# Thirty-two experts of a two-block model: one fixed stream on three engines, bias over 128 partitions, slot tables by fours

## The chip, the cores and the metric

The kernel runs on one core of one Trainium2 chip. The metric is the device time of one execution in microseconds (us); it is taken as the median of several runs. One further execution is recorded by the hardware profiler, and every row below comes from it.

## The reference, cut to what matters

The model has two blocks on 512 tokens of width 1024, in float32. The first mixes with sparse attention and a gated MLP and has a SwiGLU network; the second mixes with differential attention and a pooling mixer, then has a mixture of 32 experts, of which each token takes 4, and ends with a gated per-layer embedding. The change touches the expert stage alone:

```
logits = xt @ w_router + b_router
top_vals, top_idx = lax.top_k(logits, 4);  gates = softmax(top_vals)
# each expert e, on the rows xb of the tokens that chose it:
gt  = minimum(xb @ w_gate[e] + b_gate[e], 7.0)
up  = clip(xb @ w_up[e] + b_up[e], -7.0, 7.0)
hdn = (up + 1.0) * (gt * sigmoid(1.702 * gt))
y   = hdn @ w_down[e] + b_down[e]
# each token: sum of its four experts' rows y, weighted by gates
```

All three weights of an expert are 1024 x 1024, so the stage reads 32 x 3 x 4 MB.

## The kernel before

**Weights.** A weight of an expert comes in eight parts of 128 x 1024 (512 KB), each by one DMA on SP's queue. Products need float32 accuracy on a TensorE mode that takes a rounded operand, so every part is split (`split`, called by `load_part`; L282): ScalarE writes the rounded high half `whi` (a cast), VectorE the low half `wlo` (raw minus high). The rows `xe` (tokens) and `he` (hidden rows) are split in the same way after their transposes. `mm3` (L311 to L313) makes a product of three matmuls: high weight with high rows, low weight with high rows, high weight with low rows. A part of 1024 columns takes two halves of 512, so six matmuls.

**Buffers.** A planner (`W["plan"]`) hands out slots in rotation. At the experts there are 29 slots for raw parts and eight for halves, so the halves of a part lie in the slots of the part four before it: ScalarE's cast for part i + 4 waits until TensorE has finished the product of part i.

**An expert.** At most 112 rows (`CAP`). `prepare_slots` makes a one-hot table (`oh`, VectorE), multiplies it with the token table on TensorE and takes from the result (`sl`) the gate of each slot, and the row to gather (`gi`). `gather` fetches the rows into `xg` by an indirect DMA on POOL, `flipped` transposes and splits them. `add_bias` opens each PSUM bank with a matmul of one column of `pick`, repeated 112 times, against the bias, over 64 partitions: high and low half of the bias, 32 experts each. Gate and up parts alternate by pairs. Then the limit of the gate is taken by VectorE from PSUM in two halves (L1546, `gm`), ScalarE applies the gate function to `gm` (L1547), VectorE limits up in two halves (L1548, `uc`), and forms (up + 1) x gate (L1549). The down product of an expert is made after the gate and up products of the next; its result is scaled by ScalarE (`yt`, L1519) and added to the output rows by an indirect DMA.

**What sets the order.** Each engine works through its queue in order. The program order in the source is not that order: the Tile scheduler places each instruction by a priority and by its own estimates, so that parts of one expert mix with limits and transposes of another. Only a few places are fixed by hand with `hold`, a dependency without a semaphore.

Of the kernel before, what the change touches and what calls it, by code (L numbers as in the profile page):

```python
# [26 lines left out]
NEG = -1.0e30  # L27
NE = 32
CAP = 112
LAMBDA_INIT = 0.8 - 0.6 * math.exp(-0.3 * 0)  # L30
TWO_PI = (6.28125, 0.0019350051879882812, 3.019915981956752e-07)

# [192 lines left out]
def build(tc, I, out, dbg=None, stop=None):  # L225
# [3 lines left out]
    with es:  # L229
# [74 lines left out]
        def load_part(src, after=()):  # L304
            return start_part(src)(after)
# [1140 lines left out]
        turn = {"n": -1}  # L1446

        def part(src):
            n = turn["n"] = turn["n"] + 1
            return load_part(src, held if n <= 3 else ())  # L1450


        def expert_piece(src):
            return Piece([part(src[k * P:(k + 1) * P]) for k in range(2)])

        def expert_rows(ps, w, a, kp):
            for kk in range(2):
                k = 2 * kp + kk
                for c in range(2):
                    mm3(ps[c], (a[0][:, k], a[1][:, k]), w[kk * D + c * 512:kk * D + (c + 1) * 512], False, k == 7)  # L1460
# [9 lines left out]

        def slot_rows(pl, sl, n, bufs, m=P, norm=False):

            sg = pl.tile([P, n], F32, name="slot_gate", bufs=bufs)[:m]
            nc.vector.tensor_tensor(out=sg, in0=sl[:, :, 0], in1=sl[:, :, 1], op=ALU.add)
            rr = None
            if norm:
                rr = pl.tile([P, n], F32, name="slot_norm", bufs=1)[:m]
                nc.vector.tensor_tensor(out=rr, in0=sl[:, :, 3], in1=sl[:, :, 4], op=ALU.add)
            em = pl.tile([P, n], F32, name="empty", bufs=bufs)[:m]
            nc.vector.tensor_scalar(out=em, in0=sl[:, :, 2], scalar1=0.0, scalar2=10000.0, op0=ALU.is_equal, op1=ALU.mult)  # L1480
            gi = pl.tile([P, n], I32, name="gi", bufs=bufs)[:m]
# [3 lines left out]
        def prepare_slots(e0, n):  # L1485
            pt = ps_tr()
            for j in range(n):
                oh = one_hot(e0 + j) if e0 + j else oh0[0]
                for tt in range(NT):
                    W["pick"] = nc.tensor.matmul(pt[:CAP, 6 * j:6 * j + 6], oh[:, tt], info[:, tt, e0 + j], start=tt == 0, stop=tt == NT - 1)  # L1490
            sl = early.tile([P, n, 6], F32, name="sl", bufs=2)[:CAP]
            nc.vector.tensor_copy(sl.rearrange("p j c -> p (j c)"), pt[:CAP, :6 * n])
            *cols, last = slot_rows(early, sl, n, 6, CAP, e0 == 0)
# [4 lines left out]
        def flipped(a, name):  # L1498
# [13 lines left out]
        def down(e, he):  # L1512
            pd = [t[:CAP] for t in ps_mm()]
            add_bias(pd, e, 2)
            for kp in range(4):
                expert_rows(pd, expert_piece(I["we_down"][e, kp * 256:kp * 256 + 256]), he, kp)
            yt = row_tile("yt")[:CAP]
            last = W["mm"]
            halves(lambda cs, p: nc.scalar.activation(yt[:, cs], p, AF.Copy, scale=slots[e][0]), pd)  # L1519
            add_rows(yt, slots[e][1])  # L1520
            return last

        first = prepare_slots(0, 1)
        held = (W["gate"], first)
        normalize_first()
        prepare_slots(1, 1)

        ahead = [expert_piece(I["we_" + n][0, kp * 256:kp * 256 + 256]) for kp, n in ((0, "gate"), (0, "up"))]

        keep_warm(10, bias[:, 0, 0:P], bias[:, 0, 0:512], W["pick"])  # L1530
        xe = flipped(xg[:CAP], "xe")
        he = None
        for e in range(NE):
            if e + 1 < NE:
                gather(e + 1)
            pg, pu = [[t[:CAP] for t in ps_mm()] for _ in range(2)]
            add_bias(pg, e, 0)
            add_bias(pu, e, 1)
            for kp in range(4):
                rows = slice(kp * 256, kp * 256 + 256)  # L1540
                expert_rows(pg, ahead.pop(0) if ahead else expert_piece(I["we_gate"][e, rows]), xe, kp)
                expert_rows(pu, ahead.pop(0) if ahead else expert_piece(I["we_up"][e, rows]), xe, kp)
                if kp == 0 and e + 2 < NE:
                    prepare_slots(e + 2, 1)
            gm, uc = row_tile("gm")[:CAP], row_tile("uc")[:CAP]
            halves(lambda cs, p: nc.vector.tensor_scalar(out=gm[:, cs], in0=p, scalar1=7.0, scalar2=None, op0=ALU.min), pg)  # L1546
            nc.scalar.activation(gm, gm, AF.Gelu_apprx_sigmoid)  # L1547
            halves(lambda cs, p: nc.vector.tensor_scalar(out=uc[:, cs], in0=p, scalar1=7.0, scalar2=-7.0, op0=ALU.min, op1=ALU.max), pu)  # L1548
            nc.vector.scalar_tensor_tensor(out=uc, in0=uc, scalar=1.0, in1=gm, op0=ALU.add, op1=ALU.mult)  # L1549
            if e + 1 < NE:  # L1550
                xe = flipped(xg[:CAP], "xe")
            if he is not None:
                down(e - 1, he)
            he = flipped(uc, "he")
        last = down(NE - 1, he)
# [28 lines left out]
        def overflow_rows(op, e, r):  # L1584
# [26 lines left out]
                return t  # L1611

            def product(a, n):
                ps = [ps_b(), ps_b()]
# [35 lines left out]
        with pool("fin", 2, side="right") as wp:  # L1650
# [7 lines left out]
            for tt in range(NT):  # L1658
# [7 lines left out]
                ps = ps_mm()  # L1666
# [34 lines left out]
```

## Time and profile before

| | |
|---|---|
| median of 3 runs | 2238.23 us (2235.29 to 2238.75) |
| the profiled execution | 2236.76 us, span of its instructions 2235.0 us |
| TensorE matmul (PE) | 2156.0 us busy, 96% of the span |
| VectorE (DVE) | 1699.7 us, 76% |
| ScalarE (ACT) | 1372.4 us, 61% |
| GpSimd (POOL) | 199.2 us, 9% |
| granted TensorE clock, mean | 0.989 |

PE, DVE, ACT and POOL are the four computing engines; PEld is TensorE's weight load, which runs beside the matmuls; SP issues DMAs. A share of the span mixes stages: the first 920 us are the first block, the attention of the second block and the router; the experts take the time from about 920 to 2161 us; the gated embedding follows. So the table says which engine is busiest, not what a change in the expert stage is worth. The rows further down are taken from the expert stage alone. In a timeline row, the first number is the start in us from the beginning of the span, the second the duration (of a group: from the first start to the last end), and the square bracket tells how long the engine had been idle and what released it.

### The profile page before, as it was taken

The numbers are of one execution on the slowest core, as the hardware profiler recorded it, in microseconds if no ns is written. First come the engines' busy times: TensorE is split into PE (matmuls) and PEld (weight loads), VectorE is DVE, ScalarE is ACT, GpSimd is POOL, SyncE is SP. The second block draws the span as 40 slices with busy tenths as digits, with TensorE's granted clock in tenths as the row PEclk, the third lists the DMA queues.
The fourth block names the chain that finished last, engine by engine and source line by source line (L and its number), as shares of the span: only waits on it lengthen the run. The fifth ranks groups of instructions, "written<-read, shape, count | busy, mean of one in ns | idle before, by whom it ended". The sixth has DMA issues, their size and how long they took to land. (4 is left out here: it accounts for less than half of the span.)

```text
span 2235.0 us, 30297 instructions
## 1 busy us (share of the span) xinstructions
PE 2156.0 (96%) x10458; PEld 1658.2 (74%) x10459; DVE 1699.7 (76%) x2475; ACT 1372.4 (61%) x1873; POOL 199.2 (9%) x323
## 2 busy tenths in 40 slices
PE   9999999999999888899999999999999999999998
PEld 7777788888878777677777777777666676676667
DVE  6688772323677666799999999998888888888872
ACT  4666652222554553477777777777676676776762
POOL 0000110000003422100000000000000000000000
PEclk9999999999999999899999999999999999999999
DMA  5411744334663136799999999999999898898841
GB/s 208 152 29 37 256 151 142 94 96 159 196 204 111 29 104 220 276 348 345 359 341 362 336 361 343 356 323 348 322 330 344 300 343 323 326 345 299 309 134 67
DMA packets 159980, 543.77 MB, mean 243 GB/s; under 512 B 23107, under 2 KB 26179, under 8 KB 159820
## 3 DMA queue, kind: packets, MB, share of 16 engines
q1 hardware_dynamic: 138816, 500.63, 62.0%
q0 software_dynamic: 8192, 16.80, 3.2%
q10 hardware_dynamic: 12812, 24.35, 3.2%
q8 instruction: 84, 1.38, 0.3%
q14 instruction: 76, 0.62, 0.1%
HBM read 525.93 MB, written 28.33 MB: 248 GB/s over the span
## 5 line engine op out<-in xcount | busy, mean ns | idle before, releaser
L282 DVE TENSOR_TENSOR wlo<-wraw,whi 128x1024 fp32r<-128x1024 f32 x923 | 1096.7, 1221 | 226.7 <-ACT whi L282 209.8
L282 ACT CAST whi<-wraw 128x1024 fp32r<-128x1024 f32 x923 | 954.3, 1054 | 369.7 <-PE pa L313 122.5
L312 PE MATMUL pa<-wlo,he 128*112 128x512 f32 x504 | 202.3, 401 | 18.0 <-DVE wlo L282 18.0
L312 PE MATMUL pb<-wlo,xe 128*112 128x512 f32 x512 | 208.2, 407 | 0.0
L313 PE MATMUL pb<-whi,xe 128*112 128x512 f32 x512 | 201.3, 394 | 0.0
L313 PE MATMUL pa<-whi,he 128*112 128x512 f32 x504 | 198.0, 393 | 0.0
L311 PE MATMUL pa<-whi,he 128*112 128x512 f32 x504 | 188.5, 395 | 1.2 <-ACT he L282 1.2
L311 PE MATMUL pb<-whi,xe 128*112 128x512 f32 x512 | 185.9, 394 | 0.0
L312 PEld LDWEIGHTS pa<-wlo,he 128*112 128x112 f32 x504 | 87.9, 174 | 55.4 <-DVE wlo L282 27.0
L312 PEld LDWEIGHTS pb<-wlo,xe 128*112 128x112 f32 x512 | 89.3, 174 | 32.6 <-issue 7.9
L311 PEld LDWEIGHTS pa<-whi,he 128*112 128x112 f32 x504 | 87.7, 174 | 34.4 <-ACT whi L282 5.0
L311 PEld LDWEIGHTS pb<-whi,xe 128*112 128x112 f32 x512 | 89.4, 175 | 29.5 <-ACT xe L282 0.3
L313 PEld LDWEIGHTS pb<-whi,xe 128*112 128x112 f32 x512 | 89.4, 175 | 24.6 <-DVE xe L282 0.2
L311 PE MATMUL pa<-whi,xe 128*112 128x512 f32 x264 | 107.5, 407 | 0.0
L313 PEld LDWEIGHTS pa<-whi,he 128*112 128x112 f32 x504 | 87.9, 174 | 25.5
L312 PE MATMUL pa<-wlo,xe 128*112 128x512 f32 x264 | 106.4, 403 | 0.0
L313 PE MATMUL pa<-whi,xe 128*112 128x512 f32 x264 | 103.8, 394 | 0.0
L1509 POOL DMA_INDIRECT base<-yt,gi x32 | 47.7, 1489 | 567.7 <-DVE wlo L282 461.9
L313 PE MATMUL po<-whi,xe 128*112 128x512 f32 x248 | 97.7, 394 | 0.0
L312 PE MATMUL po<-wlo,xe 128*112 128x512 f32 x248 | 97.6, 394 | 0.0
L311 PE MATMUL po<-whi,xe 128*112 128x512 f32 x248 | 97.4, 393 | 0.0
L1418 POOL DMA_INDIRECT xg<-normed,gi x31 | 33.5, 1081 | 600.0 <-PE tr L345 570.2
(579 smaller groups left out, 4402.3 us busy)
## 6 DMA issues: line engine op xcount, KB each, us to landing
wraw<-in_we_gate_dram SPq DMA_DIRECT2D x256, 512.0 KB
wraw<-in_we_up_dram SPq DMA_DIRECT2D x256, 512.0 KB
wraw<-in_we_down_dram SPq DMA_DIRECT2D x256, 512.0 KB
wraw<-in_w_gu_dram SPq DMA_DIRECT2D x44, 512.0 KB
wraw<-in_w_down_dram SPq DMA_DIRECT2D x44, 512.0 KB
wraw<-in_w_out_dram SPq DMA_DIRECT2D x24, 512.0 KB
wraw<-in_w_v_dram SPq DMA_DIRECT2D x10, 512.0 KB
wraw<-in_w_uv_dram SPq DMA_DIRECT2D x8, 512.0 KB
```

The source lines that it names most:

```text
L282: return nc.scalar.copy(hi, src), nc.vector.tensor_tensor(out=lo, in0=src, in1=hi.bitcast(F32), op=ALU.subtract)
L311: nc.tensor.matmul(o, a[0], b[0], start=start, stop=False)
L312: nc.tensor.matmul(o, a[0], b[1], start=False, stop=False)
L313: W["mm"] = nc.tensor.matmul(o, a[1], b[0], start=False, stop=stop)
L1418: nc.gpsimd.indirect_dma_start(out=xg[:CAP], out_offset=None, in_=normed if e else base, in_offset=bass.IndirectOffsetOnAxis(ap=slots[e][1 ...
L1509: nc.gpsimd.indirect_dma_start(out=base, out_offset=bass.IndirectOffsetOnAxis(ap=ap, axis=0), in_=y_, in_offset=None, bounds_check=S - 1, ...
```

## The change

Nine things change, all in the expert stage:

1. The products are written as one sequence of parts: for each expert eight gate parts, eight up parts, then the eight down parts of the expert before. Parts are fetched so that three stand ahead of the one in use.
2. After the expert loop, every instruction of TensorE, VectorE and ScalarE of this stretch gets a dependency on the one before it on its engine (`behind`), so that the order in the source is the order in the queue.
3. `add_bias` takes all 128 partitions: `pick` has a second plane, with zeros in the partitions that belong to another bias, written by two memsets on POOL.
4. ScalarE applies the gate function directly to PSUM; the limit of the gate is put on the result, as a minimum with the function's value at 7 (`GELU_MAX`), inside the gated product.
5. The +1 of up is in its bias; its limits are then 8 and -6, taken in one instruction of 1024 columns.
6. PSUM for the experts is one pool of three tiles of 1024 columns.
7. The output rows `yt` are scaled in one instruction.
8. The slot tables of four experts are made together, with their one-hots spread over one expert's products.
9. Limits, splits of `xe` and `he` and output rows stand at fixed products q of an expert (q counts from 0 to 23).

```diff
+GELU_MAX = 7.0 / (1.0 + math.exp(-1.702 * 7.0))
...
-        pick = early.tile([P, NE], F32R, name="pick")
+        pick = early.tile([P, 2, NE], F32R, name="pick")
...
+        nc.gpsimd.memset(pick.bitcast(F32), 0.0)
+        nc.gpsimd.memset(bias[64:P, 1].bitcast(F32), 0.0)
         for q in range(4):
-            nc.vector.tensor_copy(pick[q * NE:(q + 1) * NE], ident[0:NE, 0:NE])
+            nc.vector.tensor_copy(pick[q * NE:(q + 1) * NE, q // 2], ident[0:NE, 0:NE])
...
-            nc.scalar.copy(bias[b:b + NE, h], braw)
-            nc.vector.tensor_tensor(out=bias[b + NE:b + 2 * NE, h], in0=braw, in1=bias[b:b + NE, h].bitcast(F32), op=ALU.subtract)
+            one = 1.0 if j == 1 else 0.0
+            nc.scalar.activation(bias[b:b + NE, h], braw, AF.Copy, bias=one)
+            nc.vector.scalar_tensor_tensor(out=bias[b + NE:b + 2 * NE, h], in0=braw, scalar=one, in1=bias[b:b + NE, h].bitcast(F32), op0=ALU.add, op1=ALU.subtract)
...
+        W["ps"].release()
+        W["ps"] = alloc("ps2", 1, space=PSUM)
+
+        def ps_wide():
+            return W["ps"].tile([P, D], F32, tag="w", name="pw", bufs=3)
+
+        def ps_pair():
+            t = ps_wide()
+            return [t[:, 0:512], t[:, 512:D]]
 
         def add_bias(ps, e, j):
             for c in range(2):
-                b = slice((j * 64) % P, (j * 64) % P + 64)
-                nc.tensor.matmul(ps[c], pick[b, e:e + 1].to_broadcast([64, CAP]), bias[b, j // 2, c * 512:(c + 1) * 512], start=True, stop=False)
+                nc.tensor.matmul(ps[:CAP, c * 512:(c + 1) * 512], pick[:, j % 2, e:e + 1].to_broadcast([P, CAP]), bias[:, j // 2, c * 512:(c + 1) * 512], start=True, stop=False)
 
...
+        def turned(a):
+            pts = []
+            for half in range(2):
+                pt = ps_tr()
+                for j in range(4):
+                    c = half * 4 + j
+                    nc.tensor.transpose(pt[:, j * CAP:(j + 1) * CAP], a[:, c * P:(c + 1) * P], ident[:CAP, :CAP])
+                pts.append(pt[:, :4 * CAP].rearrange("p (j t) -> p j t", j=4))
+            return pts
+        def halves_of(pts, name):
             t = [ep.tile([P, 8, CAP], F32R, name=f"{name}{q}") for q in range(2)]
-            transposed(a, t, slice(0, CAP), CAP)
+            for half, pt in enumerate(pts):
+                split(pt, *[q[:, 4 * half:4 * half + 4] for q in t])
             return t
...
+        seq = []
+        for e in range(NE):
+            seq += [("gate", e, k) for k in range(8)] + [("up", e, k) for k in range(8)]
+            seq += [("down", e - 1, k) for k in range(8)] if e else []
+        seq += [("down", NE - 1, k) for k in range(8)]
+        parts = []
+
+        def fetch(upto):
+            while len(parts) < min(upto, len(seq)):
+                n, e, k = seq[len(parts)]
+                parts.append(load_part(I["we_" + n][e, k * P:(k + 1) * P], held if len(parts) <= 3 else ()))
+
+        fetch(4)
...
+        def limited_gate():
+            hidden["g"] = row_tile("gm")[:CAP]
+            nc.scalar.activation(hidden["g"], hidden["pg"][:CAP], AF.Gelu_apprx_sigmoid)
+        def limited_up():
+            hidden["u"] = row_tile("uc")[:CAP]
+            nc.vector.tensor_scalar(out=hidden["u"], in0=hidden["pu"][:CAP], scalar1=8.0, scalar2=-6.0, op0=ALU.min, op1=ALU.max)
+        def gated_rows():
+            u = hidden["u"]
+            nc.vector.scalar_tensor_tensor(out=u, in0=hidden["g"], scalar=GELU_MAX, in1=u, op0=ALU.min, op1=ALU.mult)
+        def put_rows(e, ps):
+            yt = row_tile("yt")[:CAP]
+            nc.scalar.activation(yt, ps[:CAP], AF.Copy, scale=slots[e][0])
+            add_rows(yt, slots[e][1])
         for e in range(NE):
             if e + 1 < NE:
                 gather(e + 1)
+            batch = list(range(e + 2, min(e + 2 + NB, NE))) if e % NB == 0 else []
+            ohs, pts, pslot = {}, None, None
+            for q in range(24 if e else 16):
+                fetch(at["i"] + 4)
+                if q == 0:
+                    hidden["pg"] = ps_wide()
+                    add_bias(hidden["pg"], e, 0)
+                if q == 1 and e:
+                    operand["h"] = halves_of(turned_h, "he")
+                if q == 2 and pd is not None:
+                    put_rows(e - 2, pd)
+                    pd = None
+                if q in (0, 2, 6, 8) and len(ohs) < len(batch):
+                    ohs[len(ohs)] = one_hot(batch[len(ohs)])
+                if q in (4, 6, 10, 12):
+                    j = (4, 6, 10, 12).index(q)
+                    if j < len(batch):
+                        if j == 0:
+                            pslot = ps_tr()
+                        slot_products(pslot, j, ohs[j], batch[j])
+                if q == 13 and batch:
+                    slot_columns(pslot, batch[0], len(batch))
+                if q == 8:
+                    hidden["pu"] = ps_wide()
+                    add_bias(hidden["pu"], e, 1)
+                if q == 10:
+                    limited_gate()
+                if q == 16:
+                    pd = ps_wide()
+                    add_bias(pd, e - 1, 2)
+                if q == 17 and e + 1 < NE:
+                    operand["x"] = halves_of(pts, "xe")
+                if q == 18:
+                    limited_up()
+                if q == 19:
+                    gated_rows()
+                if q < 16:
+                    product(hidden["pg" if q < 8 else "pu"], operand["x"])
+                else:
+                    product(pd, operand["h"])
+                if q == 15 and e + 1 < NE:
+                    pts = turned(xg[:CAP])
+            if e == 0:
+                operand["x"] = halves_of(pts, "xe")
+                limited_up()
+                gated_rows()
+            turned_h = turned(hidden["u"])
...
+        behind = {}
+        for ins in list(traced[mark:]):
+            if ins.engine in ORDERED:
+                if ins.engine in behind:
+                    tc.add_manual_dep(ins, behind[ins.engine], mybir.DependencyInfo(mybir.DependencyClass.NoSync, mybir.DependencyReason.DATA), reason="order")
+                behind[ins.engine] = ins.name
...
```

On VectorE, in the middle of the expert stage, this is what stood in its queue from one expert's slot tables to the next `he` (`gm`, `uc`: gate and up rows; `wlo`: low halves of weight parts):

```order
L282 TENSOR_TENSOR wlo<-wraw,whi 128x1024 x8
L1546 TENSOR_SCALAR gm<-pa 112x512
L282 TENSOR_TENSOR wlo<-wraw,whi 128x1024
L1546 TENSOR_SCALAR gm<-po 112x512
L1548 TENSOR_SCALAR uc<-pb 112x512 x2
L282 TENSOR_TENSOR wlo<-wraw,whi 128x1024
L1549 SCALAR_TENSOR_TENSOR uc<-uc,gm 112x1024
L282 TENSOR_TENSOR xe_15734<-tr,xe_15733 128x448 x2
L282 TENSOR_TENSOR wlo<-wraw,whi 128x1024 x10
L282 TENSOR_TENSOR he_15856<-tr,he_15855 128x448 x2
```

and this stands there now (`pw` is a PSUM tile of 1024 columns):

```order
L285 TENSOR_TENSOR wlo<-wraw,whi 128x1024 x16
L285 TENSOR_TENSOR xe_15879<-tr,xe_15878 128x448 x2
L285 TENSOR_TENSOR wlo<-wraw,whi 128x1024
L1575 TENSOR_SCALAR uc<-pw 112x1024
L285 TENSOR_TENSOR wlo<-wraw,whi 128x1024
L1579 SCALAR_TENSOR_TENSOR uc<-gm,uc 112x1024
L285 TENSOR_TENSOR wlo<-wraw,whi 128x1024 x5
L1419 TENSOR_TENSOR oh<-iota,slot_of 128x448
L285 TENSOR_TENSOR wlo<-wraw,whi 128x1024
L285 TENSOR_TENSOR he_16002<-tr,he_16001 128x448 x2
```

The two gate limits are gone; the up limit and the gated product stand behind the split of `xe`, with one low half between each.

On TensorE, at the passage from one expert's up products to the down products of the expert before, these rows stood before (`tr`: transposes, `pa`, `pb`, `po`: PSUM banks of 512 columns):

```order
L311 MATMUL pb<-whi,xe_14641 112x512 x2
L1465 MATMUL pa<-bias,pick 112x512
L312 MATMUL pb<-wlo,xe_14641 112x512
L313 MATMUL pb<-whi,xe_14642 112x512
L312 MATMUL pb<-wlo,xe_14641 112x512
L313 MATMUL pb<-whi,xe_14642 112x512
L311 MATMUL pa<-whi,he_14763 112x512 x2
L1465 MATMUL po<-bias,pick 112x512
L1465 MATMUL pb<-bias,pick 112x512 x2
L312 MATMUL pa<-wlo,he_14763 112x512
```

and now:

```order
L315 MATMUL pw<-wlo,xe_15878 112x512
L316 MATMUL pw<-whi,xe_15879 112x512
L1511 MATMUL tr<-ident,xg 128x112 x8
L1467 MATMUL pw<-bias,pick 112x512 x2
L314 MATMUL pw<-whi,he_16001 112x512
L315 MATMUL pw<-wlo,he_16001 112x512
L316 MATMUL pw<-whi,he_16002 112x512
L314 MATMUL pw<-whi,he_16001 112x512
```

The biases no longer stand between a product's own matmuls; both of a tile follow the transposes or the product before.

## Rows read from the trace of the kernel before

**Rows 1.** Busy time by stretch; columns: window, length, busy us and counts of engines.

```profile
core 0: us, PE busy (x) PEld busy (x) DVE busy (x) ACT busy (x) POOL busy (x), PEclk, DMA share, GB/s
1100.00:1200.00 100.00, 100.00 (x455) 74.14 (x454) 93.81 (x104) 76.49 (x83) 5.97 (x5) 1.00 0.97 359
...
1700.00:1800.00 100.00, 97.00 (x431) 69.59 (x429) 88.19 (x99) 71.97 (x80) 6.45 (x5) 1.00 0.90 325
```

**Rows 2.** ScalarE's timeline: the gate function of three experts.

```profile
1193.82 1.06 ACT L1547 ACTIVATE gm<-gm 112x1024 f32<-112x1024 f32 x1
...
1456.12 1.05 ACT L1547 ACTIVATE gm<-gm 112x1024 f32<-112x1024 f32 x1
...
2133.70 1.06 ACT L1547 ACTIVATE gm<-gm 112x1024 f32<-112x1024 f32 x1 [4.96 <-DVE gm L1546]
```

**Rows 3.** Waits, 1500 to 2100: engine, line, releaser; total us, times, longest.

```profile
DVE gm L1546 <- PE pa L313: 37.4, 15, 2.5
...
DVE uc L1548 <- PE pb L313: 23.4, 15, 1.6
...
PE pa L312 <- DVE wlo L282: 16.3, 29, 0.7
```

**Rows 4.** VectorE's timeline around the limits of one expert, 1690 to 1702.

```profile
1691.51 0.69 DVE L1546 TENSOR_SCALAR gm<-pa 112x512 f32<-112x512 f32 x1 [2.50 <-PE pa L313]
...
1695.49 1.29 DVE L1548 TENSOR_SCALAR uc<-pb 112x512 f32<-112x512 f32 x2 [1.55 <-PE pb L313]
1696.70 1.22 DVE L282 TENSOR_TENSOR wlo<-wraw,whi 128x1024 fp32r<-128x1024 f32 x1
1697.83 1.22 DVE L1549 SCALAR_TENSOR_TENSOR uc<-uc,gm 112x1024 f32<-112x1024 f32 x1
1698.97 1.15 DVE L282 TENSOR_TENSOR xe<-tr,xe 128x448 fp32r<-128x448 f32 x2
1700.03 2.35 DVE L282 TENSOR_TENSOR wlo<-wraw,whi 128x1024 fp32r<-128x1024 f32 x2
```

**Rows 5.** TensorE's timeline behind the same limits.

```profile
1697.97 0.49 PE L312 MATMUL pa<-wlo,he 128*112 128x512 f32 x1 [0.65 <-DVE wlo L282]
1698.30 0.39 PE L313 MATMUL pa<-whi,he 128*112 128x512 f32 x1
```

**Rows 6.** TensorE's timeline at the three places of one expert's bias matmuls.

```profile
1158.81 0.72 PE L1465 MATMUL pa<-bias,pick 64*112 64x512 f32 x2
...
1159.78 0.39 PE L312 MATMUL pa<-wlo,he 128*112 128x512 f32 x1
1160.01 0.39 PE L313 MATMUL pa<-whi,he 128*112 128x512 f32 x1
...
1163.61 0.48 PE L1465 MATMUL pa<-bias,pick 64*112 64x512 f32 x1
...
1164.35 0.39 PE L313 MATMUL pa<-whi,he 128*112 128x512 f32 x1
...
1171.75 0.40 PE L313 MATMUL pa<-whi,he 128*112 128x512 f32 x1
1172.08 0.48 PE L1465 MATMUL po<-bias,pick 64*112 64x512 f32 x1
1172.08 0.72 PE L1465 MATMUL pb<-bias,pick 64*112 64x512 f32 x2
...
1173.05 0.40 PE L312 MATMUL pa<-wlo,xe 128*112 128x512 f32 x1
```

**Rows 7.** Groups by line, 850 to 2200: count, busy us, mean ns, idle before.

```profile
L282 ACT CAST whi<-wraw 128x1024 fp32r<-128x1024 f32 x770 | 794.7, 1055 | 256.8 <-PE pa L313 110.9 <-PE pb L313 55.9 <-PE po L313 55.0
...
L311 PEld LDWEIGHTS pb<-whi,xe 128*112 128x112 f32 x512 | 89.4, 175 | 29.5 <-ACT xe L282 0.3
...
L1465 PEld LDWEIGHTS pa<-bias,pick 64*112 64x112 f32 x96 | 15.2, 170 | 22.2 <-issue 12.3 <-DVE gm L1546 5.7 <-DVE wlo L282 0.4
```

**Rows 8.** VectorE's timeline in step with TensorE, 1149 to 1152.

```profile
1149.52 1.22 DVE L282 TENSOR_TENSOR wlo<-wraw,whi 128x1024 fp32r<-128x1024 f32 x1 [0.16 <-DMA wraw<-in_we_gate_dram]
1150.90 1.23 DVE L282 TENSOR_TENSOR wlo<-wraw,whi 128x1024 fp32r<-128x1024 f32 x1 [0.16 <-ACT whi L282]
```

More of the change, by code (lines that the diff above doesn't have):

```diff
@@ L29 @@
 CAP = 112
+NB = 4
+ORDERED = (mybir.EngineType.PE, mybir.EngineType.DVE, mybir.EngineType.Activation)
+GELU_MAX = 7.0 / (1.0 + math.exp(-1.702 * 7.0))
 LAMBDA_INIT = 0.8 - 0.6 * math.exp(-0.3 * 0)
@@ L1445, in build @@
         spare = W["y"] = alloc("spare", side="right")
[L1446 to L1460, printed above, removed]
+        W["ps"].release()
[5 more added lines that the diff above has]
+            return [t[:, 0:512], t[:, 512:D]]
         def add_bias(ps, e, j):
             for c in range(2):
-                b = slice((j * 64) % P, (j * 64) % P + 64)
-                nc.tensor.matmul(ps[c], pick[b, e:e + 1].to_broadcast([64, CAP]), bias[b, j // 2, c * 512:(c + 1) * 512], start=True, stop=False)
+                nc.tensor.matmul(ps[:CAP, c * 512:(c + 1) * 512], pick[:, j % 2, e:e + 1].to_broadcast([P, CAP]), bias[:, j // 2, c * 512:(c + 1) * 512], start=True, stop=False)
         def halves(f, ps):
@@ L1476, in slot_rows, with slot_products, slot_columns @@
             if norm:
-                rr = pl.tile([P, n], F32, name="slot_norm", bufs=1)[:m]
+                rr = pl.tile([P, NB], F32, name="slot_norm", bufs=1)[:m, :n]
                 nc.vector.tensor_tensor(out=rr, in0=sl[:, :, 3], in1=sl[:, :, 4], op=ALU.add)
-            em = pl.tile([P, n], F32, name="empty", bufs=bufs)[:m]
+            em = pl.tile([P, NB], F32, name="empty", bufs=bufs)[:m, :n]
             nc.vector.tensor_scalar(out=em, in0=sl[:, :, 2], scalar1=0.0, scalar2=10000.0, op0=ALU.is_equal, op1=ALU.mult)
-            gi = pl.tile([P, n], I32, name="gi", bufs=bufs)[:m]
+            gi = pl.tile([P, NB], I32, name="gi", bufs=bufs)[:m, :n]
             last = nc.vector.scalar_tensor_tensor(out=gi, in0=sl[:, :, 2], scalar=-1.0, in1=em, op0=ALU.add, op1=ALU.add)
             return sg, gi, rr, last
[L1485 to L1491, printed above, removed]
+        def slot_products(pt, j, oh, e):
+            for tt in range(NT):
+                W["pick"] = nc.tensor.matmul(pt[:CAP, 6 * j:6 * j + 6], oh[:, tt], info[:, tt, e], start=tt == 0, stop=tt == NT - 1)
+        def slot_columns(pt, e0, n):
+            sl = early.tile([P, NB, 6], F32, name="sl", bufs=2)[:CAP, :n]
             nc.vector.tensor_copy(sl.rearrange("p j c -> p (j c)"), pt[:CAP, :6 * n])
-            *cols, last = slot_rows(early, sl, n, 6, CAP, e0 == 0)
+            *cols, last = slot_rows(early, sl, n, 4, CAP, e0 == 0)
             for j in range(n):
@@ L1496, in prepare_slots @@
             return last
-        def flipped(a, name):
+        def prepare_slots(e):
+            pt = ps_tr()
+            slot_products(pt, 0, one_hot(e) if e else oh0[0], e)
+            return slot_columns(pt, e, 1)
+        def turned(a):
+            pts = []
+            for half in range(2):
+                pt = ps_tr()
+                for j in range(4):
[4 more added lines that the diff above has]
+        def halves_of(pts, name):
             t = [ep.tile([P, 8, CAP], F32R, name=f"{name}{q}") for q in range(2)]
-            transposed(a, t, slice(0, CAP), CAP)
+            for half, pt in enumerate(pts):
+                split(pt, *[q[:, 4 * half:4 * half + 4] for q in t])
             return t
@@ L1510, in add_rows @@
                                          bounds_check=S - 1, oob_is_err=False, compute_op=ALU.add)
[L1512 to L1521, printed above, removed]
@@ L1523, in build @@
-        first = prepare_slots(0, 1)
+        first = prepare_slots(0)
         held = (W["gate"], first)
         normalize_first()
-        prepare_slots(1, 1)
-        ahead = [expert_piece(I["we_" + n][0, kp * 256:kp * 256 + 256]) for kp, n in ((0, "gate"), (0, "up"))]
-        keep_warm(10, bias[:, 0, 0:P], bias[:, 0, 0:512], W["pick"])
-        xe = flipped(xg[:CAP], "xe")
-        he = None
+        prepare_slots(1)
+        seq = []
+        for e in range(NE):
+            seq += [("gate", e, k) for k in range(8)] + [("up", e, k) for k in range(8)]
+            seq += [("down", e - 1, k) for k in range(8)] if e else []
@@ new lines, in build @@
+        seq += [("down", NE - 1, k) for k in range(8)]
[5 more added lines that the diff above has]
+        fetch(4)
+        keep_warm(10, bias[:, 0, 0:P], bias[:, 0, 0:512], W["pick"])
+        operand = {"x": halves_of(turned(xg[:CAP]), "xe")}
+        traced = nc.cur_bb.bb.instructions
@@ new lines, in build, with product @@
+        mark = len(traced)
+        at = {"i": 0}
+        def product(ps, a):
+            i = at["i"]
+            k = seq[i][2]
+            w = parts[i]
+            for c in range(2):
+                cs = slice(c * 512, (c + 1) * 512)
+                mm3(ps[:CAP, cs], (a[0][:, k], a[1][:, k]), tuple(t[:, cs] for t in w), False, k == 7)
+            parts[i] = None
+            at["i"] = i + 1
+        hidden, pd = {}, None
+        def limited_gate():
+            hidden["g"] = row_tile("gm")[:CAP]
+            nc.scalar.activation(hidden["g"], hidden["pg"][:CAP], AF.Gelu_apprx_sigmoid)
@@ L1535, in build @@
                 gather(e + 1)
[L1536 to L1555, printed above, removed]
+            batch = list(range(e + 2, min(e + 2 + NB, NE))) if e % NB == 0 else []
[40 more added lines that the diff above has]
+                    pts = turned(xg[:CAP])
@@ new lines, in build @@
+            if e == 0:
[3 more added lines that the diff above has]
+            turned_h = turned(hidden["u"])
+        put_rows(NE - 2, pd)
+        operand["h"] = halves_of(turned_h, "he")
+        pd = ps_wide()
+        add_bias(pd, NE - 1, 2)
+        for q in range(8):
+            fetch(at["i"] + 4)
+            product(pd, operand["h"])
+        last = W["mm"]
+        put_rows(NE - 1, pd)
+        behind = {}
[4 more added lines that the diff above has]
+                behind[ins.engine] = ins.name
@@ L1613, in product @@
             def product(a, n):
-                ps = [ps_b(), ps_b()]
+                ps = ps_pair()
                 for k in range(8):
@@ L1665, in build @@
                     hold(nc.scalar.activation(small.tile([P, 1], F32, tag="ss", name="sgt"), mhalf[:, 0:1], AF.Sigmoid), W["square"])
-                ps = ps_mm()
+                ps = ps_pair()
                 sg = wp.tile([P, D], F32, tag="tn", name="sgm")
```

2 lines of the change are left out of this document (1 added, 1 removed).

## The prediction

> **What bounds the kernel now.** I read the utilisation table by stretch first. In the expert stage TensorE is busy 100 of 100 us early (1100 to 1200) and 97.0 late (1700 to 1800), while VectorE stands at 93.8 and 88.2, ScalarE at 76.5 and 72.0, and the DMA engines at a share of .97 and .90 [rows 1]. So TensorE sets the end, with little to spare elsewhere, and the late part loses something that the early part does not. The ScalarE timeline gives the size: the gate function runs once per expert, at 1193.82 and seven experts on at 1456.12, which is 262.30 / 7 = 37.47 us each; from there to 2133.70 are 17 more, 677.58 us or 39.86 each [rows 2]. The excess of the late part is 677.58 - 17 x 37.47 = 40.6 us.
>
> The list of waits says what it is. Between 1500 and 2100 (15 experts) VectorE waits 15 times for TensorE at the gate's limit, 37.4 us in all, and 15 times at the up limit, 23.4 us; TensorE in turn waits 29 times for a low half `wlo`, 16.3 us [rows 3]. The VectorE timeline shows the mechanism: VectorE reaches the gate limit 2.50 us before the product is finished and idles; the low halves that stand behind it in its queue wait too; then come the rest of the limits, the gated product and `xe` in a lump, up to 1700.03 [rows 4]. TensorE pays: .65 us before a `wlo` matmul at 1697.97, and the next one starts .33 after it, where .23 is usual [rows 6], so a restart costs .1 more [rows 5]. The lost 2.5 us agree in size with the 2.4 us by which the two periods differ.
>
> The second loss is in both halves. A bias matmul over 64 partitions does not keep the cadence of the others. After transposes of `xg`, two of them and their follower take 1159.78 - 1158.81 = .97 us for three slots, where the next interval is .23: .28 us too much. After those of `uc`, 1164.35 - 1163.61 = .74 us for two slots: .28 too much. In the third place two biases start at the same moment (one of `po`, one of `pb`), and from 1171.75 to 1173.05 there pass 1.30 us for five slots, .145 too much [rows 6]. Together .70 us per expert. The period then closes: 144 products and 6 biases at .231 are 34.65, two sets of eight transposes about 1.7, the slot matmuls about .4 (estimates from the same timeline), .70 for this; 37.45 against 37.47.
>
> **The change, part by part.** The sum is made on the profiled execution, 2236.76 us (span 2235.0 and 1.8 around it), which lies 1.5 under the median of the runs.
>
> *Order of the limits.* In the new order the gate function reads PSUM after product 10 of the expert (I count its 24 products from 0: gate 0 to 7, up 8 to 15, down of the expert before 16 to 23), and the up limit stands behind product 17; TensorE has finished both long before. The wait of 2.50 us goes, and with it the excess: -40.6.
>
> *Bias over 128 partitions.* Their weights load in about the time of the products' own (170 ns against 175 [rows 7]), and the products' loads lie under the running matmul. If the width is what exposes them, .70 x 31 = -21.7. The two POOL memsets that fill the zeros lie in the attention stage; I put at most 1 us on them. The bounds are 0 (width is not the cause) and -21.7; I take the upper end, since the only other difference to the products is the repeated column of `pick`, and that is the same in both kernels.
>
> In the Trainium skill ("TensorE: Matmul & The Clock Gate", section "The mechanism" of its Part 3) there is a rule that speaks against this edit: a weight load runs beside a matmul in flight only where the two use different row groups. By it, the two biases that start together in rows 6 (rows 0 to 63 and 64 to 127 of the array) are the good case, and full-width ones would be exposed. The trace does not bear out the rule for full-width products, whose 175 ns loads vanish in a cadence of 231; it does agree for the half-width ones. By the rule this term would be 0 or a small loss.
>
> *The new lump on VectorE.* Between products 17 and 20 the new order puts, behind each other: low half 20, two `xe` pieces, low half 21, the up limit in one piece, low half 22, the gated product, low half 23. From VectorE's starts [rows 4]: a low half 1.13 (1696.70 to 1697.83), the gated product 1.14, two `xe` pieces 1.06, the up limit 1.21 (two halves there, one piece now; between 1.1 and 1.25). That is 4 x 1.13 + 1.06 + 1.21 + 1.14 = 7.93 us. The lump cannot start early: high half 20 overwrites the buffers of product 16, so ScalarE begins it about .2 after product 17 starts (T), needs 1.05 [rows 7], and low half 20 starts at T + 1.28. Low half 23 ends at T + 9.2 and a handover of .05. TensorE needs it as the second matmul of product 23, at T + 6 x 1.386 + .23 = T + 8.55 (a product is six matmuls of .231). It comes .7 to .75 late; with the restart, .85 us per expert, 31 times: +26.4. Elsewhere nothing is late: in step, VectorE does one low half per 1.39 us and idles .16 of it [rows 8], and a set of transposes with two biases gives it 1.3 us more to catch up before products 16 and 0. Low half 22 is ready .13 early, the others .8 or more. The bounds: 0, if VectorE starts the lump sooner or TensorE runs a little slower; 2.24 per expert, if the buffers come free one product later (rival D). I take my count, as all durations come from rows.
>
> *What is hidden.* The gate limit's two halves leave VectorE (two of .69, [rows 4]), the slot tables' small operations fall to a quarter, the one-hots keep their number: all beside TensorE's products, worth 0 to TensorE except through the lump, where none of them stood. The +1 moves into the bias. ScalarE reads PSUM directly; at 77% it has room. On SP the weights' loads keep count and size, and the order matches the consumption; the indirect gathers and adds on POOL are as many and stand at the same distance from their users.
>
> *The ends.* Expert 0 has no down products in front of it: `xe`, up limit and gated product lie bare between product 15 and expert 1: 1.06 + ScalarE's part + 1.21 + 1.14 plus the handovers, about 4.65, of which the transposes cover .86: +3.8. The last output row copy in one piece, the start with a bias in front, and the memsets: +1.5 together (0 to 3).
>
> Sum: -40.6 - 21.7 + 26.4 + 3.8 + 1.5 = -30.6, so 2236.8 - 30.6 = 2206.2 on the profiled scale, and 2207.6 by the median. The new period would be 37.47 - .70 + .85 = 37.6 us.
>
> **Rivals.**
> - A, no lump: VectorE keeps up, the period is 36.8. For it: .75 us is a small difference of sums near 8 us. Against it: every duration in it is a row. The DMA engines do not stop it: 37.47 x .97 = 36.3 us of an expert's period are transfers now, under 36.8, though close. Time 2207.6 - 26.4 = 2181.
> - C, the biases stay exposed: the cost comes from the kind of load, not the width. For it: the load after a bias is late too, though it is a full-width one [rows 6]. Against it: full-width products are dense. Time 2207.6 + 21.7 = 2229.
> - D, slower: the ring of four parts gives its buffers back one product later than I read (TensorE's signal for product 17 instead of 16 releases high half 20). VectorE, now in fixed order, then does the lump 1.39 later, with nothing else to do in between: the stall is .85 + 1.39 = 2.24 us, 31 x 1.39 = 43 more, 2251. For it: late in the kernel before, VectorE's fixed queue cost just such an amount (2.50). Against it: the step of 1.39 in rows 8, in which each high half follows a product's end closely. It decides from a stall of .85 + 30.6 / 31 = 1.84 us per expert.
> - That the change does not do what it says is excluded by the order of the rows on VectorE and TensorE, which have the limits and biases at the stated places.
>
> **How the numbers follow.** Forecast .58, A .16, C .13, D .09, the rest (two small errors at once, or a lower TensorE clock around expert 0's bare wait) .04. A measurement of this kernel tells no less than .2%, or 4.5 us, from no change. The likeliest is 2207.5, by itself 2195 to 2220. The range takes in A and C and leaves out D: 2179 to 2236. Faster: forecast, A, most of C (2229 is 9 under the median), .86; same .05; slower .09.
>
> **What would show it.** Right: a gate function every 37.6 us through the whole stage; no wait of VectorE for TensorE at the up limit; biases at .23 intervals; one wait of TensorE for `wlo` per expert, .7 to .8 us, in the last down product, with VectorE without idle for 8 us before it. Wrong: intervals of .32 around the biases (C); no `wlo` wait (A); one of 2 us (D); waits at products other than 23, which would mean that I misread the order in which buffers come free.

## The result: 1.2% faster; the sum came out near the forecast, two of its terms did not

The changed kernel takes 2210.53 us (median of 4 runs, 2208.27 to 2211.0), the one before 2238.41 us; the ratio is 0.9877, 95% interval 0.9859 to 0.9894. The forecast was 2207.5. Two of its terms were wrong by 8 and 9 us in opposite directions, so that the sum came out right by luck.

The profiled execution has a span of 2209.3 us, where the one before had 2235.0. Split at the first matmul of an expert's weights and at the end of the last one (taken as .23 after its start):

| us | before | after | difference |
|---|---|---|---|
| up to the first expert matmul | 922.67 | 924.30 | +1.6 |
| expert stage | 1238.57 | 1202.43 | -36.1 |
| after the experts | 73.8 | 82.55 | +8.8 |

The stage lost more than forecast, and the gated embedding behind it, which the forecast did not look at, became slower. The section on the change says that all nine changes lie in the expert stage. That is not so: the diff also has this line in the gated embedding, and the same replacement in code for an expert with more than 112 tokens:

```diff
-                ps = ps_mm()
+                ps = ps_pair()
```

The utilisation by stretch in the changed kernel answers to [rows 1]: the two halves of the stage are now alike.

```profile
core 0: us, PE busy (x) PEld busy (x) DVE busy (x) ACT busy (x) POOL busy (x), PEclk, DMA share, GB/s
1100.00:1200.00 100.00, 98.18 (x448) 74.00 (x447) 88.86 (x83) 76.04 (x82) 7.12 (x5) 1.00 0.97 347
1700.00:1800.00 100.00, 98.23 (x448) 74.10 (x447) 88.67 (x83) 76.12 (x82) 7.13 (x5) 1.00 0.96 346
```

ScalarE's timeline of the gate function answers to [rows 2]. From 1011.67 to 2057.76 are 28 experts, 37.36 us each. The periods in the trace go 37.0, 37.0, 37.8, 37.8: the slot matmuls for four experts lie in the products of one, half of them before its gate function and half behind it.

```profile
1198.27 1.01 ACT L1571 ACTIVATE gm<-pw 112x1024 f32<-112x1024 f32 x1
...
1347.79 1.01 ACT L1571 ACTIVATE gm<-pw 112x1024 f32<-112x1024 f32 x1
```

The two rows are four experts apart: 149.52 us.

VectorE's timeline shows the new lump, in place of [rows 4]; no row of it waits for TensorE at a limit. The first low half (of part 20) comes after an idle time of 1.41; six more instructions (five rows) and low half 23, the first of the last group, follow without a gap.

```profile
1172.32 1.23 DVE L285 TENSOR_TENSOR wlo<-wraw,whi 128x1024 fp32r<-128x1024 f32 x1 [1.41 <-ACT whi L285]
1173.46 1.15 DVE L285 TENSOR_TENSOR xe<-tr,xe 128x448 fp32r<-128x448 f32 x2
1174.53 1.22 DVE L285 TENSOR_TENSOR wlo<-wraw,whi 128x1024 fp32r<-128x1024 f32 x1
1175.66 1.22 DVE L1575 TENSOR_SCALAR uc<-pw 112x1024 f32<-112x1024 f32 x1
1176.80 1.22 DVE L285 TENSOR_TENSOR wlo<-wraw,whi 128x1024 fp32r<-128x1024 f32 x1
1177.93 1.22 DVE L1579 SCALAR_TENSOR_TENSOR uc<-gm,uc 112x1024 f32<-112x1024 f32 x1
1179.07 5.76 DVE L285 TENSOR_TENSOR wlo<-wraw,whi 128x1024 fp32r<-128x1024 f32 x5
```

On TensorE this ends in one wait per expert, at the second matmul of product 23; it answers to [rows 5]. The first row is the start of product 17 (T in the prediction). The step 1179.33 to 1180.34 is 1.01 us, .78 more than .23, and the next one is .32: .87 together, where .85 was forecast.

```profile
1171.04 0.40 PE L314 MATMUL pw<-whi,he 128*112 128x512 f32 x1
...
1179.33 0.40 PE L314 MATMUL pw<-whi,he 128*112 128x512 f32 x1
1180.34 0.48 PE L315 MATMUL pw<-wlo,he 128*112 128x512 f32 x1 [0.61 <-DVE wlo L285]
1180.66 0.39 PE L316 MATMUL pw<-whi,he 128*112 128x512 f32 x1
```

The biases [rows 6] now keep the cadence: from 1193.64 to 1194.57 are four slots, .93.

```profile
1193.64 0.40 PE L316 MATMUL pw<-whi,xe 128*112 128x512 f32 x1
1193.88 0.62 PE L1467 MATMUL pw<-bias,pick 128*112 128x512 f32 x2
1194.34 0.39 PE L314 MATMUL pw<-whi,xe 128*112 128x512 f32 x1
1194.57 0.39 PE L315 MATMUL pw<-wlo,xe 128*112 128x512 f32 x1
```

Behind the experts the chain of waits stands on the sigmoid of the embedding. In ScalarE's timeline of the changed kernel both halves of a tile of 128 tokens come together, after 14.2 us of idle time; the split of the next tile's rows stands right behind.

```profile
2171.26 1.26 ACT L1770 ACTIVATE sgm<-pw,rstd 128x512 f32<-128x512 f32 x2 [14.22 <-issue]
2172.41 1.07 ACT L285 CAST x4T<-tr 128x512 fp32r<-128x512 f32 x2
```

In the kernel before, the first half of the second tile, of the third and of the fourth was taken while TensorE made the second half:

```profile
2199.22 0.69 ACT L1674 ACTIVATE sgm<-pa,rstd 128x512 f32<-128x512 f32 x1 [7.10 <-issue]
2204.27 0.69 ACT L1674 ACTIVATE sgm<-pa,rstd 128x512 f32<-128x512 f32 x1 [4.36 <-PE pa L313]
2204.86 1.06 ACT L282 CAST x4T<-tr 128x512 fp32r<-128x512 f32 x2
```

TensorE in the changed kernel then waits twice at each of the last three tiles, here at the second of the four, and its granted clock is .66 in the 5 us that follow (a mean of its two levels, 2.4 and 1.2 GHz):

```profile
2156.61 0.51 PE L314 MATMUL pw<-whi,x4T 128*128 128x512 f32 x1 [1.02 <-ACT x4T L285]
...
2158.69 0.61 PE L316 MATMUL pw<-whi,x4T 128*128 128x512 f32 x1 [1.34 <-DVE x4T L285]
```

```profile
2158.00:2163.00 5.00, 4.31 (x12) 3.40 (x13) 1.24 (x3) 0.00 (x0) 0.00 (x0) 0.66 0.28 105
```

The same comes again at the third tile. Nine intervals of .31 to .43 us instead of .23 at each of the two are 3.2 us, so that by this estimate over a third of the 8.8 is the lower clock behind the waits.

### The profile page after: what moved, and what is told of

Its sections match the earlier page's. It is cut to its first block, busy times and chain, and to the rows that moved or that the text cites. A ratio compares the mean times of both kernels' runs of the same rounds, so it can differ in the third digit from the quotient of the medians.

```text
span 2209.3 us, 29934 instructions
## 1 busy us (share of the span) xinstructions
PE 2116.2 (96%) x10458; PEld 1670.1 (76%) x10459; DVE 1650.9 (75%) x2291; ACT 1357.8 (61%) x1841; POOL 207.0 (9%) x325
## 5 line engine op out<-in xcount | busy, mean ns | idle before, releaser
L314 PE MATMUL pw<-whi,xe 128*112 128x512 f32 x1024 | 405.8, 396 | 0.2 <-ACT xe L285 0.2
L316 PE MATMUL pw<-whi,xe 128*112 128x512 f32 x1024 | 402.4, 393 | 1.1 <-DVE xe L285 1.1
L315 PE MATMUL pw<-wlo,xe 128*112 128x512 f32 x1024 | 402.0, 393 | 0.0
L316 PEld LDWEIGHTS pw<-whi,xe 128*112 128x112 f32 x1024 | 178.6, 174 | 60.1 <-DVE xe L285 1.6
L315 PEld LDWEIGHTS pw<-wlo,xe 128*112 128x112 f32 x1024 | 179.3, 175 | 55.6
L314 PEld LDWEIGHTS pw<-whi,xe 128*112 128x112 f32 x1024 | 178.8, 175 | 56.0 <-ACT xe L285 0.4
L315 PE MATMUL pw<-wlo,he 128*112 128x512 f32 x512 | 203.4, 397 | 18.1 <-DVE wlo L285 18.1
L314 PE MATMUL pw<-whi,he 128*112 128x512 f32 x512 | 202.0, 394 | 0.4 <-ACT he L285 0.4
L316 PE MATMUL pw<-whi,he 128*112 128x512 f32 x512 | 201.0, 393 | 0.0
L315 PEld LDWEIGHTS pw<-wlo,he 128*112 128x112 f32 x512 | 89.3, 174 | 61.9 <-DVE wlo L285 36.5
L314 PEld LDWEIGHTS pw<-whi,he 128*112 128x112 f32 x512 | 89.2, 174 | 29.2 <-ACT he L285 0.8
L316 PEld LDWEIGHTS pw<-whi,he 128*112 128x112 f32 x512 | 89.3, 174 | 26.3 <-DVE he L285 0.4
L314 PE MATMUL pa<-x2T,whi 128*128 128x512 f32 (+1 forms) x200 | 72.6, 364 | 0.1
L315 PE MATMUL pa<-x2T,whi 128*128 128x512 f32 (+1 forms) x200 | 72.7, 364 | 0.0
L316 PE MATMUL pa<-x2T,wlo 128*128 128x512 f32 (+1 forms) x200 | 72.6, 363 | 0.0
```

## The experiments

All times are medians of 4 or 5 runs; the kernel before, on the same chips, stood at 2237.6 to 2238.5.

**Two PSUM tiles in the embedding.** The changed kernel with:

```diff
-            t = ps_wide()
-            return [t[:, 0:512], t[:, 512:D]]
+            return [ps_wide()[:, 0:512] for _ in range(2)]
```

> The changed kernel with the gated embedding's product in two PSUM tiles again, one for each half of 512 columns; the expert stage is untouched. Theory (the shared tile costs the tail): from the last expert matmul to the end the changed kernel takes 82.6 us where the kernel before took 73.8, because the sigmoid of the first half waits for both halves when they lie in one tile; the tail falls to 73 to 75 us, the time by 8 to 9, to about 2202. Rival (the tail is longer for another reason, such as when its rows are loaded): time stays at 2210, and VectorE and ScalarE still idle 12 to 14 us between the tiles of 128 tokens.

Measured: 2200.70 us (ratio to before 0.9835, 0.9819 to 0.9852), 9.8 less than the changed kernel. The part after the experts is 74.0 us. ScalarE takes the first half early again:

```profile
2163.39 0.69 ACT L1769 ACTIVATE sgm<-pw,rstd 128x512 f32<-128x512 f32 x1 [7.09 <-issue]
2168.44 0.69 ACT L1769 ACTIVATE sgm<-pw,rstd 128x512 f32<-128x512 f32 x1 [4.36 <-PE pw L316]
```

So the shared tile is the whole loss behind the experts (8.6 of 8.8): in this kernel a reader of one half waits for the last writer of the tile, also if that one wrote the other half.

**Bias over 64 partitions in the changed kernel.**

```diff
-nc.tensor.matmul(ps[...], pick[:, j % 2, e:e + 1].to_broadcast([P, CAP]), bias[:, j // 2, ...])
+b = slice((j * 64) % P, (j * 64) % P + 64)
+nc.tensor.matmul(ps[...], pick[b, j % 2, e:e + 1].to_broadcast([64, CAP]), bias[b, j // 2, ...])
```

> The changed kernel with bias matmuls over 64 partitions as before, all else kept. Theory (the width exposes the loads): intervals of .32 us around the biases come back, .5 to .7 us per expert, +15 to +22, 2226 to 2232. Rival C (the kind of load, not its width): intervals and time as in the changed kernel, 2210, within 3 us.

Measured: 2245.35 us (1.0039, 1.0024 to 1.0053), slower than the kernel before, and 34.8 more than the changed kernel. The direction was that of the theory, the size over its end. From 1161.85 to 1163.37 five intervals take 1.52 us, .37 more than five of .23:

```profile
1161.85 0.40 PE L316 MATMUL pw<-whi,xe 128*112 128x512 f32 x1
1162.17 0.71 PE L1468 MATMUL pw<-bias,pick 64*112 64x512 f32 x2
1162.81 0.49 PE L314 MATMUL pw<-whi,xe 128*112 128x512 f32 x1
1163.14 0.39 PE L315 MATMUL pw<-wlo,xe 128*112 128x512 f32 x1
1163.37 0.39 PE L316 MATMUL pw<-whi,xe 128*112 128x512 f32 x1
```

The other two pairs of an expert stand behind transposes and cost .36 each, .16 of it in the interval before the pair. Three pairs are 1.1 us, and the mean period is 1.10 longer (38.45 against 37.35, from the second gate function on).

The rows of TensorE's weight loads (PEld) show where the time goes. In the changed kernel (first fence) the load of a bias starts at 1193.64, together with the matmul before its own, and is done when its own starts. With 64 partitions the load of the first bias, and that of the product behind the pair, start .32 us after the matmul before, at the same moment as their own matmul:

```profile
1193.64 0.41 PEld L1467 LDWEIGHTS pw<-bias,pick 128*112 128x112 f32 x2
```

```profile
1162.17 0.27 PEld L1468 LDWEIGHTS pw<-bias,pick 64*112 64x112 f32 x2 [0.38 <-issue]
1162.81 0.17 PEld L314 LDWEIGHTS pw<-whi,xe 128*112 128x112 f32 x1 [0.38 <-issue]
```

**Bias over 128 partitions in the kernel before**, as its only change (the same lines the other way round, with the two memsets).

> The kernel before with the bias over 128 partitions as its only change. Theory: the .70 us per expert go in the early half, where the period falls from 37.47 to about 36.8; in the late half VectorE's wait at the gate limit may keep a part; 12 to 22 us less than before, 2216 to 2226. Rival C: no change, 2238.

Measured: 2207.25 us (0.9866, 0.9849 to 0.9882), 31 less than before: this edit alone gives as much as all of the change. The early period falls from 37.5 to 36.6, the late one from 40.0 to 38.9. That is .85 and 1.1 per expert, more than the expected range; rival C falls. The gate function of expert 7, seven experts on, and of the last:

```profile
1189.33 1.05 ACT L1548 ACTIVATE gm<-gm 112x1024 f32<-112x1024 f32 x1
...
1445.68 1.05 ACT L1548 ACTIVATE gm<-gm 112x1024 f32<-112x1024 f32 x1
...
2104.99 1.06 ACT L1548 ACTIVATE gm<-gm 112x1024 f32<-112x1024 f32 x1 [4.26 <-DVE gm L1547]
```

From the first of eight transposes to the bias behind them pass .87 us in the kernel before (first fence) and .70 in this run:

```profile
1157.94 0.93 PE L345 MATMUL tr<-ident,xg 112*128 112x112 f32 x8
1158.81 0.72 PE L1465 MATMUL pa<-bias,pick 64*112 64x512 f32 x2
```

```profile
1154.35 0.93 PE L345 MATMUL tr<-ident,xg 112*128 112x112 f32 x8
1155.05 0.69 PE L1466 MATMUL pa<-bias,pick 128*112 128x512 f32 x2
```

VectorE's wait at the gate limit stays in the late half (the waits between 1000 and 2050):

```profile
DVE gm L1547 <- PE pa L313: 31.8, 15, 2.1
```

**The limits earlier.** In the changed kernel:

```diff
-                if q == 17 and e + 1 < NE:
+                if q == 16 and e + 1 < NE:
                     operand["x"] = halves_of(pts, "xe")
-                if q == 18:
+                if q == 16:
                     limited_up()
-                if q == 19:
+                if q == 18:
                     gated_rows()
```

> The changed kernel with the split of xe and the up limit one and two products earlier (both at product 16) and the gated product at 18, so that VectorE does them while it idles for high half 20. Theory (a lump on VectorE costs .87 us per expert): no wait for a low half at product 23, the mean period falls from 37.4 to 36.5, 27 us less, about 2183. Rival (what bounds the period is the weights' transfers, at a share of .97 to .99 in the changed kernel): the period falls to 37.0 at most, the waits for low halves turn into waits for weights, time 2197 or more. Second rival (the lump only moves): a wait of about the same size at product 20 or 21, 2210.

Measured: 2183.05 us (0.9758, 0.9742 to 0.9774), 27.5 less than the changed kernel, at the expected number. The list of TensorE's waits between 1000 and 2050 is empty, the mean period is 36.44 (29 experts between the two rows), and the transfers did not stop it, though their share is now .99:

```profile
973.95 1.02 ACT L1571 ACTIVATE gm<-pw 112x1024 f32<-112x1024 f32 x1
...
2030.82 1.02 ACT L1571 ACTIVATE gm<-pw 112x1024 f32<-112x1024 f32 x1
```

```profile
1100.00:1200.00 100.00, 100.00 (x464) 76.70 (x463) 89.38 (x83) 78.49 (x84) 7.12 (x5) 1.00 0.99 361
```

So the lump cost what the row count said, and it filled idle time when its pieces stood one or two products sooner.

**Without the fixed order.** The changed kernel without the `behind` loop.

> The changed kernel without the loop that fixes the order of the three engines; the scheduler places the instructions, from the new program text. Theory (the fixed order is what keeps a limit from blocking the queue behind it): in a part of the stage VectorE waits 1 to 2.5 us per expert for TensorE at a limit again, and the period there is 38.5 to 40; time 2215 to 2250. Rival (the new text alone removes the wait, since the gate's limit has left VectorE): no such wait, 2200 to 2212.

Measured: 2199.71 us (0.9828, 0.9812 to 0.9845). The time is near the rival's (just under its range), 10.8 less than with the fixed order, but the mechanism is that of the theory: from the third to the fourteenth the periods are 36.07 and 36.9, as dense as with the limits earlier, and from the sixteenth on they are 37.2 to 38.9, with VectorE waiting at a limit 15 times (25.3 us). From the list of waits between 1000 and 2050, and two rows of VectorE's timeline:

```profile
DVE uc L1575 <- PE pw L316: 25.3, 15, 2.0
```

```profile
1701.94 8.04 DVE L285 TENSOR_TENSOR wlo<-wraw,whi 128x1024 fp32r<-128x1024 f32 x7 [2.68 <-ACT whi L285]
1711.55 1.22 DVE L1575 TENSOR_SCALAR uc<-pw 112x1024 f32<-112x1024 f32 x1 [1.57 <-PE pw L316]
```

So the scheduler's placement is better than the written one early and worse late, and the written one is better than both once the lump is gone (2183). My theory overrated the fixed order. The new program text alone takes VectorE's wait at the gate limit of [rows 3] away (ScalarE, which now has the gate function, waits 16 times for TensorE there, 33.2 us) and leaves VectorE's wait at the up limit. What is left costs about 1.2 per expert in the late half, 19 us by this estimate, less than the lump's 27.7 over the whole stage.

**The gate's limit on VectorE again.** The changed kernel with:

```diff
-            nc.scalar.activation(hidden["g"], hidden["pg"][:CAP], AF.Gelu_apprx_sigmoid)
+            nc.vector.tensor_scalar(out=hidden["g"], in0=hidden["pg"][:CAP], scalar1=7.0, ..., op0=ALU.min)
+            nc.scalar.activation(hidden["g"], hidden["g"], AF.Gelu_apprx_sigmoid)
```

> The changed kernel with the limit of the gate back on VectorE, in one piece of 1024 columns at product 10, and the gate function from its result. Theory (where the limit stands matters, not that it is done): VectorE has idle time at products 9 to 16, so 2210, within 3 us. Rival (VectorE's load decides): 1.2 us more per expert on VectorE, a part of which reaches TensorE, 2220 to 2245.

Measured: 2249.94 us (1.0057, 1.0041 to 1.0074), 39 more than the changed kernel. My theory failed, and the time lies above the rival's range too. ScalarE waits for VectorE, which first makes a low half; the next casts stand behind it in ScalarE's queue:

```profile
1168.78 1.06 ACT L1572 ACTIVATE gm<-gm 112x1024 f32<-112x1024 f32 x1 [2.43 <-DVE gm L1571]
1169.74 4.85 ACT L285 CAST whi<-wraw 128x1024 fp32r<-128x1024 f32 x5
```

TensorE then waits at an up product for a low half, .77 at 1172.08 in this trace, besides the wait at product 23. To tell the load of VectorE from the handover, the gate function alone moves by two products, into a function of its own (shown in part):

```diff
                 if q == 10:
                     limited_gate()          # the limit, on VectorE
+                if q == 12:
+                    gate_function()         # on ScalarE
```

> As the run with the gate's limit on VectorE, but ScalarE takes the gate function two products later (at product 12), so that no cast of a weight part waits behind it for VectorE. Theory (the handover costs, not VectorE's 1.2 us: ScalarE waits 2.4 us for the limit and the casts behind it come late): 2210, within 4 us, and no wait of ScalarE for the limit. Rival (VectorE's load costs): 2240 or more, as with the function at product 10.

Measured: 2212.02 us (0.9882, 0.9865 to 0.9898), 1.5 from the changed kernel. ScalarE no longer waits:

```profile
1164.07 1.05 ACT L285 CAST whi<-wraw 128x1024 fp32r<-128x1024 f32 x1 [0.33 <-PE pw L316]
1165.03 1.06 ACT L1574 ACTIVATE gm<-gm 112x1024 f32<-112x1024 f32 x1
```

VectorE's 1.2 us were free; the handover between two queues in fixed order, without distance, cost 37.9 us over the stage.

**Both repairs**, the limits earlier and two PSUM tiles.

> Both repairs together: xe, up limit and gated product earlier, and two PSUM tiles in the gated embedding. Theory (they lie in different stages): 2183.05 - 9.8 = 2173, within 2 us. Rival: the earlier end of the experts takes cover from the embedding's loads, so that a part of the 9.8 is lost: 2176 to 2183.

Measured: 2172.70 us (0.9708, 0.9692 to 0.9724). The two add up.

**The passage from expert 0**, on top of both repairs.

```diff
+                if q == 4 and e == 1:
+                    turned_h = turned(hidden["u"])
-                if q == 1 and e:
+                if q == (5 if e == 1 else 1) and e:
                     operand["h"] = halves_of(turned_h, "he")
...
-                if q == 15 and e + 1 < NE:
+                if q == (15 if e else 13) and e + 1 < NE:
                     pts = turned(xg[:CAP])
...
-            turned_h = turned(hidden["u"])
+            else:
+                turned_h = turned(hidden["u"])
```

> The two repairs, and in expert 0 alone the transposes of the next rows two products earlier and those of its hidden rows after four products of expert 1, so that TensorE waits only for the split of xe. Theory (in the changed kernel TensorE idles 4.7 us there, and its clock is then at half for some 4 us, which costs 2 more): 1.5 us of idle time are left and the clock stays up, 5 us less than the two repairs alone, about 2168. Rival (the clock falls all the same, or VectorE is late for the next products): 1 to 3 us less, 2170 to 2172.

Measured: 2169.61 us (0.9693, 0.9677 to 0.971), the best of all; 3.1 less than both repairs, just under the rival's range, with medians uncertain by about 1.5. The expected 5 us were not reached. In the changed kernel TensorE waited 4.47 for the gated rows, and its clock stood at .50 from 955 to 960:

```profile
955.39 1.73 PE L1511 MATMUL tr<-ident,uc 112*128 112x112 f32 x8 [4.47 <-DVE uc L1579]
```

```profile
955.00:960.00 5.00, 4.61 (x16) 3.77 (x17) 1.38 (x2) 0.00 (x0) 0.00 (x0) 0.50 0.87 288
```

That wait is gone, two of 1.40 and .44 have come (the first for a PSUM tile that the slot table still held), and the clock stays up there. In this trace the first expert's start was slower, with the clock at .68 from 925 to 930; whether by the edit or by chance is open.

## Why the forecast came out right

The sum came out by luck: the bias saved 8 us more than its term, and the embedding took 9 that no term had. The lump was forecast rightly, mechanism and size. In spans, forecast and measured side by side:

| term | forecast | measured | from |
|---|---|---|---|
| bias over 128 partitions | -21.7 | -29.6 | stage of before, with and without that edit |
| lump on VectorE | +26.4 | +27.7 | stage of the changed kernel, with and without the earlier limits |
| order of the limits and passage from expert 0 (-40.6 + 3.8) | -36.8 | -34.2 | stage of the earlier limits (1174.7) against before with bias over 128 (1208.9): what is left of the stage |
| the ends | +1.5 | +10.4 | start and embedding in the table at the top |
| sum | -30.6 | -25.7 | spans of the profiled executions; the medians differ by 27.9 |

The split depends on where a term is measured. In the changed kernel, with and without the narrow bias, the stage differs by 34.4; with that for the bias, the third row would be -29.4.

- *Order of the limits, -40.6, and the passage, +3.8.* The wait of [rows 3] is gone; its own size was not measured alone. With bias over 128 partitions the excess of the late part is 37 us by the three gate functions shown above (256.35 / 7 = 36.62 early, 659.31 / 17 = 38.78 late); the other 4 of the 40.6 were the narrow bias, which cost more late than early. The passage from expert 0 cost more than +3.8: to its 4.5 us of bare wait come, at half clock, eight transposes of .19 in place of .10 and eight matmuls of .43 in place of .23, with the biases between them 2.5 us in all. What is left of the row, some -4, is not assigned to a cause.
- *Bias.* The mechanism was right (the width exposes the loads), the term too small by 8 us. The step that failed is the reading of [rows 6]: I began at the bias's own start. The interval before it is long too: .19 from the last transpose to the bias, where a full-width one follows after .03, and I had booked that with the transposes. In the new order there is also no pair that starts at the same moment, so the narrow bias would have cost 1.1 us per expert, not .70. The rule of the Trainium skill on row groups ("TensorE: Matmul & The Clock Gate", section "The mechanism" of its Part 3) was weighed as a reason against; the full-width biases of the changed kernel run at .23 behind a product, and behind transposes two of them take .33 together (.03 and .30), so the measurement decides against it here.
- *Lump.* Every step held: low half 20 at T + 1.28 (forecast 1.28), 7.9 us from it to the end of low half 23, .78 late (forecast .7 to .75), .87 with the restart. Rivals A and D fall by this trace.
- *Hidden.* That the gate limit's removal is worth nothing was half right: its 1.2 us on VectorE are free (the run with a distance of two products), but the handover that it needs is not where it has no distance (37.9 us).
- *The ends, +1.5.* This is the term that failed. The diff replaces `ps_mm()` by `ps_pair()` in the embedding, and I read it as another name for two PSUM halves. One tile for both makes the first sigmoid wait for the second half: +8.8, or 9.8 by the runs.

## What to carry to other kernels

When an order is written by hand, count the low-priority pieces between two deadlines in the rows and start them in the idle time before the first; here one or two products earlier were worth 27.5 us. A handover between two engines whose order is fixed needs distance: none cost 37.9 us, two products made it free, and one was not tried. A buffer made wider to save instructions can bind all its readers to its last writer, as here: look at every user of a helper that the diff replaces, also outside the stage that the change is about. A sum that comes out right is no proof of its terms.

## What was not expected of the hardware

- A pair of matmuls over 64 partitions between ones over 128 costs about .09 us at each of four intervals: into the pair, inside it, out of it, and at the following one (.32, .32, .32, .33 against .23). The width decides, and at each change of it a weight load no longer lies under the matmul before it; why it does not is open.
- With the transfers at a share of .99 and 361 GB/s, TensorE still had no wait in 1000 us. It can't be told from these runs how much of that share was needed.
